# Layer step on one core: FFN sums and splits in another place, attention scores over 128 rows, sample keys and values as fp32 weights

## The chip, the cores and the metric

The kernel runs on one core of one Trainium2 chip. Its metric is the device time of one execution in microseconds (us). Before the change it takes 1013.33 us (median of three runs, 1012.04 to 1014.15).

## The reference

One inference step of a decoder layer with D = 1024, for a prompt of 512 tokens and 8 samples of one token each (520 columns in all):

```
x += 0.5 * (silu(h @ w1) * (h @ w3)) @ w2        # h = rmsnorm(x), hidden width 2816
z  = rmsnorm(x) @ w_in                           # conv gate b, c, x_in; attention q, k, v
y_c = b * causal_conv(c * x_in)                  # 512 channels
y_a = sum over 3 dilated windows, joint softmax of q k / 8, times v   # 8 heads x 64
x += concat(rmsnorm(y_c), rmsnorm(y_a)) @ w_out
x += 0.5 * (silu(h @ w1') * (h @ w3')) @ w2'
y  = rmsnorm(x)
```

A sample attends to 256 cached rows that the windows reach, and to itself; its keys and values come from the caches (`cache_k`, `cache_v`). The caches are also copied to the outputs, shifted by one row. All is fp32, and the products must keep fp32 accuracy.

## The kernel before, in words

Activations lie transposed: 128 channels on the partitions, the 520 tokens along the free axis, in two halves of 260. A large product is made from three fp32r matmuls (`mm3`, L121 to L123): both operands are split into a rounded part and a remainder (hi and lo), and hi·hi, hi·lo and lo·hi are added in PSUM. A weight block is loaded by `load_w` (L95): SyncE issues the DMA into one of four buffers `raw`, ScalarE rounds it to `hi` (L108), VectorE subtracts to get `lo` (L109). TensorE works nearly all the time; the other engines prepare operands for it.

The stages in order: first feed-forward block (0 to 380 us), mixer (380 to 644 us: projections, prompt heads, convolution, samples, output projection), second feed-forward block (644 to 1000 us), final norm.

*Feed-forward block* (`ffn`). Four hidden blocks m = 0 to 3 are made one by one from the split input `xh`, `xl` (the loop at L286): two products, the gate on ScalarE, `b` on VectorE (L302, L303), and the split into `hh` (ScalarE, L305) and `hl` (VectorE, L306). Then `down` (L311) multiplies them by w2 for the eight output blocks. After it come pairs of hidden blocks by `seven`, which needs sums of quarters of x: `x_sums(k)` (L350) makes, for k = 0 to 3, a tile `z` (names f0z, f1z; L355 to L359), its rounded part `sh` (ScalarE, L362) and its remainder `sl` (VectorE, L363, 128x1820). Two of the four calls, k = 0 and 1, stand behind m = 1 and m = 2 (L308); the other two, k = 2 and 3, stand inside the `down` loop (L311 to L314). A scheduler with a model of times puts the instructions of one engine in order; it may take work that is ready ahead of work that stands earlier in the code.

*Prompt heads* (`head`, L578). For each of eight heads, four blocks of 128 queries are multiplied by up to 512 keys. q is split into q2 (both halves of the 128 rows hold its 64 rounded rows) and ql (64 rows of remainder); k2 holds k's rounded rows in the head's half and its remainder in the other. One matmul over 128 rows gives q_hi·k_hi + q_hi·k_lo; a second one over 64 rows adds q_lo·k_hi (L589). The eight matmuls are kept in a fixed order.

*Samples.* Scores (`sample_scores`): for each of 8 samples the keys are loaded and split by `load_w`; the samples' queries stand in `sqm`, zero-padded 128x128 blocks that GpSimd fills and clears (L687, L689), as weights. 32 matmuls with 256 columns (L694) and 32 of 64 weight columns (L695) add all samples into one PSUM tile. Values (`sample_out`): the same with the probabilities as weights and the split values as the moving side, 16 + 16 matmuls of 512 columns (L741, L742), four transposes (L752), and sums into `AS` (L758, L759). Then `rstd_rows` (L813) and the second half of the output projection follow, which need the samples' result.

The order of the mixer's steps is the string `ORDER` (L33).

Of the kernel before, what the change touches and what calls it, by code (L numbers as in the profile page):

```python
# [16 lines left out]
B = 8  # L17
# [15 lines left out]
ORDER = ("A0 C00 C01! k1 q1 q2 B0 v1 v2 t1 C02 A1! B1! k3 k2 t2 A2 v3 C10 C11 q3 B2 t3 A3 C12 "  # L33
# [18 lines left out]
def tile_step(ctx: ExitStack, tc: tile.TileContext, xT, w0, w1a, w3a, w2a, w_in, w_out, w1b, w3b, w2b,  # L52
# [148 lines left out]
    def x_operand(pool, name, col, start):  # L201

        xh, xl = [], []
        for k in range(KD):
            h = pool.tile([P, T], F32R, name=f"{name}h{k}", tag=f"xh{k}")
            l = pool.tile([P, T], F32R, name=f"{name}l{k}", tag=f"xl{k}")
            for c in ([slice(0, TH), slice(TH, T)] if start and not k else [slice(0, T)]):
                scaled_split(X[k][:, c], h[:, c], l[:, c], col + k)
            xh.append(h)
            xl.append(l)  # L210
# [12 lines left out]
        A.activation(s, X[KD - 1], AF.Square)  # L223
        return xh, xl, sums + [s]

    def ffn(i, w1, w3, w2, g, psum, finish=None):
# [17 lines left out]
        with ExitStack() as st, ExitStack() as sx:  # L244
# [4 lines left out]
            with tc.tile_pool(name=f"xa{i}", bufs=1, side="right", reuse_waits="tile") as xa, \  # L249
# [36 lines left out]
                for m in range(CUTS[1]):  # L286
# [18 lines left out]
                    A.activation(hh, b, AF.Copy)  # L305
                    V.tensor_tensor(hl, b, hh.bitcast(F32), ALU.subtract)  # L306
# [170 lines left out]
    with ExitStack() as st:  # L477
# [9 lines left out]
        with ExitStack() as s2:  # L487
# [44 lines left out]

            qk, vs, vv = {}, {}, {}
# [23 lines left out]
            def do_q(hp):  # L557
                q = rotate(project(12 + hp), "q")
                G.tensor_copy(QS[:, hp], q[:, S:])
                q2 = [ap.tile([P, S], F32R, name=f"q2{e}", tag=f"q2{e}", bufs=2) for e in range(2)]  # L560
                ql = ap.tile([P, S], F32R, name="ql", tag="ql", bufs=2)
                for e in range(2):
                    for f in range(2):
                        A.activation(q2[e][ROWS[f]], q[ROWS[e], :S], AF.Copy)
                    V.tensor_tensor(ql[ROWS[e]], q[ROWS[e], :S], q2[e][ROWS[e]].bitcast(F32), ALU.subtract)
                qk["q", hp] = q2, ql
# [11 lines left out]
            def head(e, q2, ql, k2, v2, at):  # L578
# [5 lines left out]

                for at_, (ib, low) in enumerate(((0, 0), (1, 0), (0, 1), (1, 1), (2, 1), (2, 0), (3, 0), (3, 1))):
                    n = max(256, P * (ib + 1))
                    i = slice(ib * P, (ib + 1) * P)
                    one = ib < 2
                    mm = PE.matmul(dst[ib], lhsT=ql[rows, i] if low else q2[e][:, i], rhs=k2[e][rows if low else slice(0, P), :n],  # L589
                                   start=at_ in (0, 4, 6), stop=one or at_ in (5, 7), skip_group_check=one and at_ > 0)  # L590
                    if at_ not in (0, 6):
                        tc.keep_in_program_order(mm)
# [68 lines left out]
            def padded(n):  # L661

                z = [ap.tile([P, HP * 130 + 64], F32R, name=f"sqm{i}", tag=f"sqm{i}") for i in range(2)]
                for t in z:
                    G.memset(t[:, :n].bitcast(F32), 0.0)
                return z

            def sample_scores():
                zeros = padded(HP * 130 + 64)
# [6 lines left out]
                qs = ap.tile([P, B, HP, 2, 2], F32R, name="sqs", tag="sqs")  # L676
                A.activation(qs[:, :, :, 0], q2, AF.Copy)
                V.tensor_tensor(qs[:, :, :, 1], q2, qs[:, :, :, 0].bitcast(F32), ALU.subtract)
                sc = psS.tile([P, 512], F32, name="sc", tag="x", bufs=1)
                for b in range(B):  # L680
                    hi, lo = load_w(ckT[b], KD)
                    qf = zeros[b % 2]
                    for a in range(b % 2, b + 1, 2):
                        own = qf[:, NH * a:NH * a + 130 * HP].rearrange("p (h c) -> p h c", h=HP)[:, :, :P]
                        own = own.rearrange("p h (l c) -> p h l c", l=2)[:, :, :, :2]
                        if a == b:
                            G.tensor_copy(own, qs[:, b])  # L687
                        elif a == b - 2:
                            G.memset(own.bitcast(F32), 0.0)  # L689
                    qm = qf[:, :P * HP].rearrange("p (h l c) -> p h l c", h=HP, l=2)  # L690
                    for hp in range(HP):
                        k = slice(2 * hp, 2 * hp + 2)
                        end = b == B - 1 and hp == HP - 1
                        mm = [lambda: PE.matmul(sc[:, :256], lhsT=qm[:, hp], rhs=hi[:, k], start=b == 0 and hp == 0, stop=end),  # L694
                              lambda: PE.matmul(sc[:64, :256], lhsT=qm[:, hp, 0], rhs=lo[:, k], start=False, stop=False)]  # L695
                        for f in (mm[::-1] if end else mm):
                            f()
                    if b % 2 and b < B - 1:
                        yield
                PE.matmul(sc[:64, 256:257], lhsT=kq.rearrange("p b h e -> p (b h e)"), rhs=ones[:, 0:1], start=True, stop=True)  # L700
                got["sc"] = sc
                yield

            def sample_softmax(sc):
                ss = ap.tile([64, 257], F32, name="ss", tag="p2")
                V.memset(ss[:, 256:257], 0.0)
                A.activation(ss[:, :256], sc[64:, :256], AF.Copy)
                V.tensor_tensor(ss, sc[:64, :257], ss, ALU.add)
# [3 lines left out]
                V.tensor_tensor_reduce(out=pr, in0=ss, in1=smk, op0=ALU.add, op1=ALU.min, scale=-0.125, scalar=-NEG, accum_out=mx)  # L712
# [9 lines left out]
                return tp, pn  # L722

            def sample_out():
                tp, pn = got['m']
                zeros = padded(256)
                ps_ = ap.tile([P, 2, 2, 64], F32R, name="sps", tag="sqs")
                A.activation(ps_[:, :, 0], tp[:, :2], AF.Copy)
                V.tensor_tensor(ps_[:, :, 1], tp[:, :2], ps_[:, :, 0].bitcast(F32), ALU.subtract)
                so = psS.tile([P, 512], F32, name="so", tag="x", bufs=1)  # L730
                for b in range(B):
                    hi, lo = load_w(cvg[b], KD)
                    pz = zeros[b % 2][:, :256].rearrange("p (j l c) -> p j l c", j=2, l=2)
                    if b > 1:
                        G.memset(pz[:, :, :, NH * (b - 2):NH * (b - 1)].bitcast(F32), 0.0)
                    c = slice(NH * b, NH * (b + 1))
                    G.tensor_copy(pz[:, :, :, c], ps_[:, :, :, c])
                    for j in range(2):
                        k = slice(HP * j, HP * (j + 1))
                        end = b == B - 1 and j == 1  # L740
                        mm = [lambda: PE.matmul(so, lhsT=pz[:, j], rhs=hi[:, k], start=b == 0 and j == 0, stop=end),  # L741
                              lambda: PE.matmul(so[:64], lhsT=pz[:, j, 0], rhs=lo[:, k], start=False, stop=False)]  # L742
                        for f in (mm[::-1] if end else mm):
                            f()
# [5 lines left out]
                ot = psS.tile([P, 512], F32, name="ot", tag="s")  # L750
                for hp in range(HP):
                    PE.transpose(ot[:, 64 * hp:64 * hp + 64], os_[:, hp * P:(hp + 1) * P], ident[:64, :64])  # L752
                PE.matmul(ot[:, 320:384], lhsT=ones[:1, :], rhs=pn, start=True, stop=True)
                new = ot[:, 320:384].rearrange("p (b h e) -> p b h e", b=B, h=HP)
                own = ot[:, :66 * HP].rearrange("p (h c) -> p h c", h=HP)
                for e in range(2):
                    r = ROWS[e]
                    V.tensor_tensor(AS[r], new[r, :, :, e].rearrange("p b h -> p h b"), VS[r], ALU.mult)  # L758
                    V.tensor_tensor(AS[r], own[r, :, e:e + 8 * B - 7:8], AS[r], ALU.add)  # L759
# [26 lines left out]
            def go(step):  # L786
# [9 lines left out]
                elif what == "M":  # L796
                    got["m"] = sample_softmax(got["sc"])
# [165 lines left out]
```

## Time and profile before

| | |
|---|---|
| time, median of three runs | 1013.33 us (1012.04 to 1014.15) |
| the profiled execution | 1013.21 us, its span 1011.4 us |
| TensorE matmuls busy | 979.8 us, 97% of the span |
| weight loads busy | 956.2 us, 95% |
| VectorE busy | 719.8 us, 71% |
| ScalarE busy | 519.3 us, 51% |
| GpSimd busy | 69.5 us, 7% |
| mean DMA rate | 135 GB/s |

TensorE's matmuls are pipelined, so that their durations overlap: a matmul of 260 columns lasts 0.28 us in the profile, but the next starts 0.12 us after it. Costs on TensorE are therefore read from start to start. PEclk is the clock granted to TensorE, 1.00 for 2.4 GHz and 0.50 for 1.2 GHz. The fp32 matmuls (not fp32r) have two records each in the profile: the code's line 86 runs 8 of them at the start, and the profile counts 16.

### The profile page before, as it was taken

To read this page: it belongs to the slowest core of one execution; us is meant where nothing else is said; L and a number is where in the kernel's file an instruction comes from. 1 tells how busy PE (TensorE), PEld (TensorE's weight loads), DVE (VectorE), ACT (ScalarE), POOL (GpSimd) and SP (SyncE) were. 2 spreads that over 40 slices of the span, in tenths; PEclk is the share of its full clock that TensorE was granted. 3 is DMA by queue.
4 is the path that set the end of the run, shared out by engine and by line. 5 is a ranking of instruction groups with operands and counts; after the bars stand their busy time and mean duration, and the time that the engine had idled before them with its cause. 6 is when DMAs were issued, how large, how long until landed. Compare 5 with 4: busy or idle time off the path is not lost.

```text
span 1011.4 us, 19194 instructions
## 1 busy us (share of the span) xinstructions
PE 979.8 (97%) x7897; PEld 956.2 (95%) x7897; DVE 719.8 (71%) x1153; ACT 519.3 (51%) x941; POOL 69.5 (7%) x89
## 2 busy tenths in 40 slices
PE   8979999999999998999999999999999999999997
PEld 8979999999999998999999999999999999999997
DVE  7878888435886437676788889797898633788433
ACT  5535565423565325676476555453566522565442
POOL 1000000000000031111122220000000000000022
PEclk9989999999999999999999999999999999999998
DMA  7324434354444434233245466325444223333302
GB/s 240 109 93 168 146 135 143 108 179 168 147 146 146 138 134 164 105 127 130 102 146 209 159 223 223 116 93 168 145 146 147 60 87 125 106 100 110 105 21 86
DMA packets 37912, 136.62 MB, mean 135 GB/s; under 512 B 5760, under 2 KB 8512, under 8 KB 37312
## 3 DMA queue, kind: packets, MB, share of 16 engines
q1 hardware_dynamic: 37824, 135.39, 39.6%
q8 instruction: 62, 1.02, 0.4%
q14 instruction: 26, 0.21, 0.1%
HBM read 131.07 MB, written 37.82 MB: 167 GB/s over the span
## 4 chain that ended last, share of the span: by engine, by line
PE 75%; DVE 7%; issue 2%; DMA 2%; ACT 1%; POOL 1%; POOLq 0%; DVEq 0%; ACTq 0%
PE ps L121 24%; PE ps L123 23%; PE ps L122 23%; PE s L589 1%; DVE lo L390 1%; DVE lo L109 1%; DMA raw<-in_w1a 1%; PE pt L610 1%; DVE ls L390 1%; DMA raw<-in_w3a 1%; PE o L619 0%; ACT hi L108 0%; DVE raw L377 0%; ACT hi L389 0%; PE so L741 0%
## 5 line engine op out<-in xcount | busy, mean ns | idle before, releaser
L108 ACT ACTIVATE hi<-raw 128x1024 fp32r<-128x1024 f32 (+3 forms) x136 | 119.0, 878 | 214.2 <-PE ps L122 158.4
L121 PE MATMUL ps<-hh,hi 128*128 128x260 f32 x704 | 199.5, 286 | 5.6 <-ACT hh L305 3.1
L122 PE MATMUL ps<-hl,hi 128*128 128x260 f32 x704 | 199.2, 284 | 3.8 <-DVE hl L306 3.8
L123 PE MATMUL ps<-hh,lo 128*128 128x260 f32 x704 | 200.0, 285 | 2.8 <-DVE lo L109 2.8
L109 DVE TENSOR_TENSOR lo<-raw,hi 128x1024 fp32r<-128x1024 f32 (+3 forms) x136 | 138.6, 1020 | 74.4 <-ACT hi L108 73.3
L121 PEld LDWEIGHTS ps<-hh,hi 128*128 128x128 f32 x704 | 133.1, 190 | 7.4 <-ACT hh L305 3.5
L122 PEld LDWEIGHTS ps<-hl,hi 128*128 128x128 f32 x704 | 133.4, 190 | 4.5 <-DVE hl L306 4.5
L123 PEld LDWEIGHTS ps<-hh,lo 128*128 128x128 f32 x704 | 133.2, 189 | 3.9 <-DVE lo L109 3.4
L121 PE MATMUL ps<-mh,hi 128*128 128x260 f32 x384 | 110.0, 287 | 3.4 <-ACT mh L135 1.6
L122 PE MATMUL ps<-ml,hi 128*128 128x260 f32 x384 | 109.4, 285 | 0.8 <-DVE ml L136 0.8
L123 PE MATMUL ps<-mh,lo 128*128 128x260 f32 x384 | 109.1, 284 | 0.1
L389 ACT ACTIVATE hi<-raw 128x512 fp32r<-128x512 f32 x144 | 82.5, 621 | 35.9 <-PE ps L122 26.6
L390 DVE TENSOR_TENSOR lo<-raw,hi 128x1024 fp32r<-128x1024 f32 x72 | 87.7, 1218 | 5.3 <-ACT hi L389 4.8
L121 PE MATMUL ps<-f0sh,hi 128*128 128x260 f32 x288 | 81.5, 284 | 1.4 <-ACT hi L389 1.0
L121 PE MATMUL ps<-f1sh,hi 128*128 128x260 f32 x288 | 81.3, 283 | 0.4 <-ACT a L401 0.3
L123 PE MATMUL ps<-f0sh,lo 128*128 128x260 f32 x288 | 80.7, 284 | 0.9 <-DVE lo L390 0.7
L123 PE MATMUL ps<-f1sh,lo 128*128 128x260 f32 x288 | 80.9, 284 | 0.1
L122 PE MATMUL ps<-f0sl,hi 128*128 128x260 f32 x288 | 81.0, 282 | 0.0
L122 PE MATMUL ps<-f1sl,hi 128*128 128x260 f32 x288 | 81.0, 282 | 0.0
L144 POOL TENSOR_TENSOR acc<-acc,sq 128x520 f32<-128x520 f32 (+1 forms) x19 | 28.7, 1511 | 750.4 <-ACT sq L143 750.4
L121 PEld LDWEIGHTS ps<-mh,hi 128*128 128x128 f32 x384 | 72.2, 188 | 4.8 <-ACT mh L135 1.9
L122 PEld LDWEIGHTS ps<-ml,hi 128*128 128x128 f32 x384 | 72.3, 188 | 2.2 <-DVE ml L136 1.0
(278 smaller groups left out, 2660.2 us busy)
## 6 DMA issues: line engine op xcount, KB each, us to landing
out_cko<-in_ck SPq DMA_DIRECT2D x16, 1023.0 KB, 6.1
out_cvo<-in_cv SPq DMA_DIRECT2D x16, 1023.0 KB, 7.6
raw<-in_w_in SPq DMA_DIRECT2D x24, 512.0 KB, 3.3
raw<-in_w1b SPq DMA_DIRECT2D x22, 512.0 KB, 3.3
raw<-in_w3b SPq DMA_DIRECT2D x22, 512.0 KB, 3.3
raw<-in_w3a SPq DMA_DIRECT2D x21, 512.0 KB, 3.3
raw<-in_w1a SPq DMA_DIRECT2D x20, 512.0 KB, 3.3
raw<-in_w2a SPq DMA_DIRECT2D x16, 320.0 KB, 3.0
```

Of the source, the lines that this page charges most:

```text
L108: A.activation(hi, raw, AF.Copy)
L109: V.tensor_tensor(lo, raw, hi.bitcast(F32), ALU.subtract)
L121: PE.matmul(out, lhsT=hi, rhs=xh, start=start, stop=False, skip_group_check=more)
L122: PE.matmul(out, lhsT=hi, rhs=xl, start=False, stop=False, skip_group_check=more)
L123: PE.matmul(out, lhsT=lo, rhs=xh, start=False, stop=stop, skip_group_check=more)
L144: eng.tensor_tensor(dst[:, c], dst[:, c], sq[:, c], ALU.add)
L389: A.activation(h[:, c:c + KQ], f[:, c:c + KQ], AF.Copy)
L390: V.tensor_tensor(l, f, h.bitcast(F32), ALU.subtract)
L589: mm = PE.matmul(dst[ib], lhsT=ql[rows, i] if low else q2[e][:, i], rhs=k2[e][rows if low else slice(0, P), :n], start=at_ in (0, 4, 6), s ...
L610: PE.transpose(t[:, o + ib * P:o + (ib + 1) * P], pr[ib][:, jb * P:(jb + 1) * P], ident)
```

## The change

There are four parts.

1. In `x_operand` the tiles of the split input are allocated ahead of their use, in reversed order.
2. In `ffn`, the sums of x for k = 2 and 3 are issued after both halves of the last hidden split (m = 3) instead of wherever the scheduler finds room.
3. In `head`, the remainder matmul runs over 128 rows. Four tiles `rest` hold ql in one half and zeros (written once) in the other. The matmuls of one block of queries stand next to each other, without a kept order. In `ORDER`, B0 moves ahead of q2.
4. In the samples, keys and values are used as they come from the DMA, as fp32 weights (128x128 blocks of `raw`), with two moving columns (the two heads of a pair) each: 64 matmuls for the scores (8 samples x 4 pairs x 2 halves), 64 for the values. `load_w`, the padded tiles on GpSimd and the split of the probabilities go. The scores come out transposed: two transposes turn them back, and the values need none.

```diff
-ORDER = ("A0 C00 C01! k1 q1 q2 B0 v1 v2 t1 ...
+ORDER = ("A0 C00 C01! k1 q1 B0 q2 v1 v2 t1 ...
...
     def x_operand(pool, name, col, start):
-        xh, xl = [], []
+        xs = [[pool.tile([P, T], F32R, name=f"{name}{x}{k}", tag=f"x{x}{k}") for x in "hl"] for k in range(KD)[::-1]]
+        xh, xl = zip(*xs[::-1])
...
                     hh, hl = hidden(m)
-                    A.activation(hh, b, AF.Copy)
-                    V.tensor_tensor(hl, b, hh.bitcast(F32), ALU.subtract)
+                    made = [A.activation(hh, b, AF.Copy), V.tensor_tensor(hl, b, hh.bitcast(F32), ALU.subtract)]
...
                     if then:
-                        then()
+                        with tc.issue_after(made[0].ins), tc.issue_after(made[1].ins):
+                            then()
...
+            rest = [[ap.tile([P, S], F32R, name=f"ql{i}{e}") for e in range(2)] for i in range(2)]
+            for r in rest:
+                for e in range(2):
+                    V.memset(r[e][ROWS[1 - e]].bitcast(F32), 0.0)
...
-                for at_, (ib, low) in enumerate(((0, 0), (1, 0), (0, 1), (1, 1), (2, 1), (2, 0), (3, 0), (3, 1))):
+                for ib in range(4):
                     n = max(256, P * (ib + 1))
                     i = slice(ib * P, (ib + 1) * P)
-                    mm = PE.matmul(dst[ib], lhsT=ql[rows, i] if low else q2[e][:, i], rhs=k2[e][rows if low else slice(0, P), :n],
...
+                    PE.matmul(dst[ib], lhsT=q2[e][:, i], rhs=k2[e][:, :n], start=True, stop=False)
+                    PE.matmul(dst[ib], lhsT=ql[e][:, i], rhs=k2[e][:, :n], start=False, stop=True)
...
+            def cache(src):
+                raw = wp.tile([P, KD, P], F32, name="raw", tag="raw", bufs=4)
+                load(raw, src)
+                return raw
...
                 for b in range(B):
-                    hi, lo = load_w(ckT[b], KD)
...
+                    raw = cache(ckT[b])
                     for hp in range(HP):
...
-                        mm = [lambda: PE.matmul(sc[:, :256], lhsT=qm[:, hp], rhs=hi[:, k], start=b == 0 and hp == 0, stop=end),
-                              lambda: PE.matmul(sc[:64, :256], lhsT=qm[:, hp, 0], rhs=lo[:, k], start=False, stop=False)]
+                        for j in range(2):
+                            PE.matmul(sc[:, j, b, hp], lhsT=raw[:, 2 * hp + j], rhs=q2[:, b, hp], start=True, stop=True)
...
+                for j in range(2):
+                    PE.transpose(ss[:64, j * P:(j + 1) * P], st[:, j], ident)
...
-                        mm = [lambda: PE.matmul(so, lhsT=pz[:, j], rhs=hi[:, k], start=b == 0 and j == 0, stop=end),
-                              lambda: PE.matmul(so[:64], lhsT=pz[:, j, 0], rhs=lo[:, k], start=False, stop=False)]
+                    raw = cache(cvg[b])
+                    for hp in range(HP):
+                        for j in range(2):
+                            PE.matmul(so[:, j, b, hp], lhsT=raw[:, HP * j + hp], rhs=pj[:, j, b, hp], start=True, stop=True)
...
-                os_ = ap.tile([64, 512], F32, name="os_", tag="u")
-                A.activation(os_, so[64:], AF.Copy)
-                V.tensor_tensor(os_, so[:64], os_, ALU.add)
...
-                    V.tensor_tensor(AS[r], own[r, :, e:e + 8 * B - 7:8], AS[r], ALU.add)
+                    for j in range(2):
+                        V.tensor_tensor(AS[r], so[r, j, :, :, e].rearrange("p b h -> p h b"), AS[r], ALU.add)
```

The lines of the changed kernel have other numbers: in the loop of the hidden blocks they are lower by 2 or 3 (L306 is L303), the scores stand in L591 and L592, the samples' products in L678 and L715.

The order of VectorE where the first feed-forward block ends its hidden blocks; hl_581 is the remainder of m = 2, hl_711 that of m = 3, f0sl the remainders of the sums. Before:

```order
L303 TENSOR_TENSOR b<-b,a 128x520
L358 SCALAR_TENSOR_TENSOR f0z<-f0z 128x260 x2
L359 SCALAR_TENSOR_TENSOR f0z<-f0z 128x260 x2
L306 TENSOR_TENSOR hl_581<-b,hh_580 128x520
L302 TENSOR_TENSOR b<-ps,rbc 128x520
L303 TENSOR_TENSOR b<-b,a 128x520
L363 TENSOR_TENSOR f0sl_753<-f0z,f0sh_752 128x1820
L363 TENSOR_TENSOR f0sl_828<-f0z,f0sh_827 128x1820
L306 TENSOR_TENSOR hl_711<-b,hh_710 128x520
```

And of the changed kernel:

```order
L301 TENSOR_TENSOR b<-b,a 128x520
L109 TENSOR_TENSOR lo<-raw,hi 128x512
L303 TENSOR_TENSOR hl_581<-b,hh_580 128x520
L300 TENSOR_TENSOR b<-ps,rbc 128x520
L301 TENSOR_TENSOR b<-b,a 128x520
L303 TENSOR_TENSOR hl_711<-b,hh_710 128x520
L353 SCALAR_TENSOR_TENSOR f0z<-X_70,gv,rbc 128x520
L353 SCALAR_TENSOR_TENSOR f0z<-X_66,gv,rbc 128x520
L353 SCALAR_TENSOR_TENSOR f0z<-X_71,gv,rbc 128x520
L353 SCALAR_TENSOR_TENSOR f0z<-X_67,gv,rbc 128x520
```

The making of the sums and their two long remainders stood ahead of hl_711; now all of it stands behind hl_711, and the remainders come between the updates of X in `down`.

The order of TensorE at the scores of the first head; s01, s2 and s3 are PSUM tiles. Before, with the 64-row matmuls reading ql:

```order
L589 MATMUL s01_4681<-k20_4661,q20_4592 128x256 x2
L589 MATMUL s01_4681<-k20_4661,ql_4594 128x256 x2
L589 MATMUL s2_4682<-k20_4661,ql_4594 128x384
L589 MATMUL s2_4682<-k20_4661,q20_4592 128x384
L589 MATMUL s3_4683<-k20_4661,q20_4592 128x512
L589 MATMUL s3_4683<-k20_4661,ql_4594 128x512
```

And of the changed kernel, where ql00 has 128 rows:

```order
L591 MATMUL s01_4688<-k20_4668,q20_4600 128x256
L592 MATMUL s01_4688<-k20_4668,ql00_4479 128x256
L591 MATMUL s01_4688<-k20_4668,q20_4600 128x256
L592 MATMUL s01_4688<-k20_4668,ql00_4479 128x256
L591 MATMUL s2_4689<-k20_4668,q20_4600 128x384
L592 MATMUL s2_4689<-k20_4668,ql00_4479 128x384
L591 MATMUL s3_4690<-k20_4668,q20_4600 128x512
L592 MATMUL s3_4690<-k20_4668,ql00_4479 128x512
```

The same eight products remain; the two kinds alternate, and none has fewer than 128 rows.

The order of TensorE at the end of the samples' values; so is the PSUM tile of the result, sqm the padded probabilities, raw the loaded values. Before:

```order
L742 MATMUL so_6700<-lo_6970,sqm0_6693 64x512
L741 MATMUL so_6700<-hi_6969,sqm0_6693 128x512
L742 MATMUL so_6700<-lo_6970,sqm0_6693 64x512
L741 MATMUL so_6700<-hi_6981,sqm1_6694 128x512
L619 MATMUL o_6801<-pth0_4469,v2_6030 128x512
```

And of the changed kernel, where spj holds the probabilities:

```order
L715 MATMUL so_6647<-spj_6582,raw_6885 128x2 x5
L715 MATMUL so_6647<-spj_6582,raw_6895 128x2 x5
L618 MATMUL o_6746<-ptl3_4476,v2_6034 64x256
L619 MATMUL o_6746<-pth3_4472,v2_6034 128x256
L715 MATMUL so_6647<-spj_6582,raw_6895 128x2 x3
L715 MATMUL so_6647<-spj_6582,raw_6905 128x2 x8
L715 MATMUL so_6647<-spj_6582,raw_6915 128x2 x8
L719 MATMUL ot_6925<-spn_6580,ones_73 128x64
```

A few products of 512 columns between others have become a run of 29 products of two columns. Elsewhere the changed order has such runs of 16 (scores), 16 and 2 (values, followed by the five products of L193), and 17 among transposes. Behind ot, the changed order has 35 matmuls of the output projection ahead of the norm that needs the samples; before it has 72 of them.

## Rows read from the trace of the kernel before

**Rows 1.** The page's first section: busy time, share of the span, instructions of each engine

```profile
PE 979.8 (97%) x7897; PEld 956.2 (95%) x7897; DVE 719.8 (71%) x1153; ACT 519.3 (51%) x941; POOL 69.5 (7%) x89
```

**Rows 2.** Busy time by stretch; columns: stretch, length, engines, clock, DMA share, GB/s

```profile
412.00:600.00 188.00, 187.36 (x1429) 174.82 (x1429) 145.96 (x308) 116.20 (x221) 32.96 (x55) 1.00 0.44 152
```

**Rows 3.** TensorE in order of time, first feed-forward block; columns: start, us, work, [idle before]

```profile
59.28 0.62 PE L121 MATMUL ps<-hh,hi 128*128 128x260 f32 x3 [1.14 <-ACT hh L305]
60.57 0.39 PE L122 MATMUL ps<-hl,hi 128*128 128x260 f32 x1 [0.67 <-DVE hl L306]
63.51 1.02 PE L121 MATMUL ps<-hh,hi 128*128 128x260 f32 x3 [1.95 <-ACT hh L305]
66.58 0.59 PE L122 MATMUL ps<-hl,hi 128*128 128x260 f32 x1 [2.05 <-DVE hl L306]
```

**Rows 4.** VectorE in order of time, the same stretch

```profile
61.90 4.01 DVE L363 TENSOR_TENSOR f0sl<-f0z,f0sh 128x1820 fp32r<-128x1820 f32 x2
65.83 0.69 DVE L306 TENSOR_TENSOR hl<-b,hh 128x520 fp32r<-128x520 f32 x1
70.02 0.70 DVE L427 SCALAR_TENSOR_TENSOR X<-ps,X 128x520 f32<-128x520 f32 x1 [3.50 <-PE ps L123]
```

**Rows 5.** TensorE in order of time, the same place of the second block

```profile
683.88 0.39 PE L123 MATMUL ps<-hh,lo 128*128 128x260 f32 x1 [1.57 <-DVE lo L109]
686.46 0.39 PE L122 MATMUL ps<-hl,hi 128*128 128x260 f32 x1 [1.10 <-DVE hl L306]
```

**Rows 6.** VectorE in order of time, just before

```profile
683.75 2.05 DVE L363 TENSOR_TENSOR f1sl<-f1z,f1sh 128x1820 fp32r<-128x1820 f32 x1
```

**Rows 7.** TensorE in order of time, the scores of one head

```profile
417.45 0.40 PE L589 MATMUL s<-k,q 128*128 128x256 f32 x2
418.98 0.50 PE L589 MATMUL s<-k,ql 64*128 64x512 f32 x1
419.40 0.39 PE L121 MATMUL ps<-mh,hi 128*128 128x260 f32 x1
```

**Rows 8.** TensorE in order of time, sample values and projection

```profile
590.15 0.40 PE L741 MATMUL so<-hi,sqm 128*128 128x512 f32 x1
590.38 0.39 PE L742 MATMUL so<-lo,sqm 128*64 128x512 f32 x1
592.70 0.28 PE L121 MATMUL ps<-Yh,hi 128*128 128x260 f32 x1
592.82 0.28 PE L122 MATMUL ps<-Yl,hi 128*128 128x260 f32 x1
```

**Rows 9.** Waits of the removed line 741

```profile
  POOL sqm L737: 0.8, 2
```

**Rows 10.** TensorE in order of time, fp32 products

```profile
573.88 1.08 PE L193 MATMUL nps<-ones,acc 128*104 128x1 f32 x10 [0.20 <-POOL acc L144]
574.81 0.37 PE L589 MATMUL s<-k,q 128*128 128x256 f32 x1
999.99 1.05 PE L86 MATMUL ps<-ones 128*128 128x128 f32 x8
1000.88 0.58 PE L839 MATMUL nps<-ones,acc 128*65 128x1 f32 x8
```

**Rows 11.** Busy time by stretch where the clock fell

```profile
60.00:63.40 3.40, 0.99 (x6) 0.78 (x6) 3.33 (x4) 3.40 (x3) 0.00 (x0) 1.00 0.05 19
66.80:70.20 3.40, 3.40 (x16) 3.40 (x17) 0.18 (x1) 0.35 (x1) 0.00 (x0) 0.50 0.00 0
1002.10:1005.50 3.40, 3.10 (x29) 2.91 (x30) 0.99 (x6) 0.87 (x3) 0.00 (x0) 1.00 0.61 202
1005.50:1008.90 3.40, 0.84 (x5) 0.65 (x4) 1.75 (x6) 0.39 (x1) 1.42 (x2) 0.50 0.63 215
```

**Rows 12.** VectorE and ScalarE in order of time, end of the samples

```profile
600.53 0.20 DVE L759 TENSOR_TENSOR AS<-ot,AS 64x32 f32<-64x32 f32 x1
603.51 0.64 ACT L171 ACTIVATE rhi<-acc_a 128x520 fp32r<-128x520 f32 x1 [0.32 <-POOL acc_a L144]
```

More of the change, by code (lines that the diff above doesn't have):

```diff
@@ L560, in do_q @@
                 q2 = [ap.tile([P, S], F32R, name=f"q2{e}", tag=f"q2{e}", bufs=2) for e in range(2)]
-                ql = ap.tile([P, S], F32R, name="ql", tag="ql", bufs=2)
+                ql = rest[hp % 2]
                 for e in range(2):
@@ L675, in sample_scores @@
                 V.tensor_tensor(kq, q2, KS.rearrange("p h b -> p b h").unsqueeze(3).to_broadcast([P, B, HP, 2]), ALU.mult)
[L676 to L679, printed above, removed]
+                sc = psS.tile([P, 2, B, HP, 2], F32, name="sc", tag="x", bufs=1)
@@ L680, in sample_scores @@
                 for b in range(B):
-                    hi, lo = load_w(ckT[b], KD)
[L682 to L689, printed above, removed]
@@ L698, in sample_scores, with sample_softmax @@
+                    for hp in range(HP):
+                        for j in range(2):
+                            PE.matmul(sc[:, j, b, hp], lhsT=raw[:, 2 * hp + j], rhs=q2[:, b, hp], start=True, stop=True)
                     if b % 2 and b < B - 1:
                         yield
-                PE.matmul(sc[:64, 256:257], lhsT=kq.rearrange("p b h e -> p (b h e)"), rhs=ones[:, 0:1], start=True, stop=True)
-                got["sc"] = sc
+                got["sc"] = sc, kq
                 yield
[L704 to L708, printed above, removed]
+            def sample_softmax(sc, kq):
+                st = ap.tile([P, 2, 64], F32, name="st", tag="p2")
+                A.activation(st, sc.rearrange("p j b h e -> p j (b h e)"), AF.Copy)
+                ss = psS.tile([P, 512], F32, name="ss", tag="s")
+                for j in range(2):
+                    PE.transpose(ss[:64, j * P:(j + 1) * P], st[:, j], ident)
+                PE.matmul(ss[:64, 256:257], lhsT=kq.rearrange("p b h e -> p (b h e)"), rhs=ones[:, 0:1], start=True, stop=True)
@@ L721, in sample_softmax @@
                 V.tensor_copy(pn, tp[:1, 2])
-                return tp, pn
+                pj = ap.tile([P, 2, B, HP, 2], F32, name="spj")
+                V.tensor_copy(pj.rearrange("p j b h e -> p j (b h e)"), tp[:, :2])
+                return pj, pn
             def sample_out():
[L725 to L729, printed above, removed]
@@ L730, in sample_out @@
-                so = psS.tile([P, 512], F32, name="so", tag="x", bufs=1)
-                for b in range(B):
[L732 to L740, printed above, removed]
-                        mm = [lambda: PE.matmul(so, lhsT=pz[:, j], rhs=hi[:, k], start=b == 0 and j == 0, stop=end),
-                              lambda: PE.matmul(so[:64], lhsT=pz[:, j, 0], rhs=lo[:, k], start=False, stop=False)]
-                        for f in (mm[::-1] if end else mm):
-                            f()
+                pj, pn = got['m']
@@ L748, in sample_out @@
-                A.activation(os_, so[64:], AF.Copy)
-                V.tensor_tensor(os_, so[:64], os_, ALU.add)
[L750 to L754, printed above, removed]
@@ L755, in sample_out @@
-                own = ot[:, :66 * HP].rearrange("p (h c) -> p h c", h=HP)
+                ot = psS.tile([P, B, HP, 2], F32, name="ot", tag="s")
+                PE.matmul(ot.rearrange("p b h e -> p (b h e)"), lhsT=ones[:1, :], rhs=pn, start=True, stop=True)
                 for e in range(2):
                     r = ROWS[e]
-                    V.tensor_tensor(AS[r], new[r, :, :, e].rearrange("p b h -> p h b"), VS[r], ALU.mult)
-                    V.tensor_tensor(AS[r], own[r, :, e:e + 8 * B - 7:8], AS[r], ALU.add)
+                    V.tensor_tensor(AS[r], ot[r, :, :, e].rearrange("p b h -> p h b"), VS[r], ALU.mult)
+                    for j in range(2):
+                        V.tensor_tensor(AS[r], so[r, j, :, :, e].rearrange("p b h -> p h b"), AS[r], ALU.add)
@@ L796, in go @@
                 elif what == "M":
-                    got["m"] = sample_softmax(got["sc"])
+                    got["m"] = sample_softmax(*got["sc"])
                 elif what == "V":
```

28 lines of the change are left out of this document (5 added, 23 removed).

## The prediction

> **What bounds the kernel now.** I read the page's busy line first, then busy time by stretch, then TensorE in order of time wherever a stretch is not full. TensorE's matmuls are busy 979.8 of 1011.4 us [rows 1], and in the mixer's middle, where most of the change lies, 187.36 of 188.00 us at a granted clock of 1.00, while VectorE has 145.96 and ScalarE 116.20 [rows 2]. So a change there is worth what it does to TensorE's own list, from start to start; work taken off ScalarE, VectorE and GpSimd (32 splits of the samples' keys and values, the padded tiles) is worth nothing, being hidden by that list, except where TensorE waited for it. A GEMM matmul of 260 columns costs 0.12 us and one of 512 columns 0.23 us [rows 8].
>
> The visible holes in TensorE's time lie at the end of the hidden blocks. In the first feed-forward block TensorE waits 1.14, 0.67, 1.95 and 2.05 us, for hh and hl [rows 3]. The VectorE rows say why: two long remainders f0sl, 4.01 us, start at 61.90, and hl of the last hidden block gets its turn only at 65.83 [rows 4]. TensorE worked 0.99 us of 60.00 to 63.40, and the granted clock then stood at 0.50, that is 1.2 GHz: 66.80 to 70.20 holds 16 matmuls [rows 11], where 3.40 us at 0.12 us would hold 28. In the second block the waits are 1.57 and 1.10 us [rows 5], again with a 2.05 us remainder just ahead of hl [rows 6], and without a fall of the clock.
>
> **The change, part by part.** The sum is made against the profiled execution, 1013.21 us (a span of 1011.4 and 1.8 around it), 0.1 below the median of 1013.33.
>
> *Part 1* only changes where tiles lie: 0.
>
> *Part 2, first block.* The four waits make 5.81 us, and I add an estimated 1.2 us for refilling the pipeline behind each (0.39 instead of 0.28 us for the first matmul [rows 3, 7], some 0.3 us for each start that was late). The slow clock costs (28 - 16) x 0.12 = 1.5 us. That is 8.5 us. In the new order hl of m = 3 follows directly on its product b, with no remainder between. I expect it done near 59.9, with about 1 us of waiting left for the chain product, gate, split. Gain 7.5. If the new order only shortens the last two waits (4.0 us) it is 4; if nothing is left waiting it is 8.5. The moved work, about 9 us of VectorE (four products for the sums, four 260- or 520-column passes, 4.01 us of remainders), needs cover: VectorE idles 3.50 us until 70.02 in the down stage [rows 4], and the rest must fit between the updates of X, before the pairs need the sums. That is tight, so I put 0.3 us of new waits against it, with 0 and 3 as ends.
>
> *Part 2, second block.* 1.57 + 1.10 = 2.67 us, with the refills 3.0; 0.3 stays. Gain 2.7 (1 to 3). Together part 2 gives -7.5 - 2.7 + 0.3 = -9.9 us.
>
> *Part 3.* One head's scores take from 417.45 to 419.40, and the GEMM behind them another 0.11 us more than usual: 2.06 us. The 64-row matmul of 512 columns alone takes 0.42 us until the next start [rows 7] against 0.23 us for 512 columns elsewhere [rows 8]. Eight 128-row matmuls at the usual pace are 4 x 0.12 + 2 x 0.175 + 2 x 0.23 = 1.29 us (0.175 for 384 columns lies between the two measured). So -0.77 us per head and, for eight heads, -6.2 us. Ends: 0, if the alternation keeps the cost, and -7. The zeros are written once on VectorE, four passes over 64 rows, beside a full TensorE: 0. The Trainium skill (TensorE: Matmul & The Clock Gate, section "Why this matters for your kernels") holds that a single matmul over few rows takes the same time as one over 128; by that rule this part would give 0 and the sum below would be 6.2 us higher. The row disagrees: 0.42 against 0.23 us.
>
> *Part 4, TensorE.* Removed are 64 matmuls of 256 columns and 32 of 512: 64 x 0.12 + 32 x 0.23 = 15.0 us, and the wait of 0.8 us for GpSimd's padded tile [rows 9]. Added are 128 fp32 matmuls with 128 weight columns and two moving columns, each with two records. No row shows exactly this. The nearest is L193, fp32 with 104 weight columns and one moving column: ten records from 573.88 to 574.81, 0.093 us each; by weight columns that makes 0.114. L86, 128 weight columns, takes 0.89 / 8 = 0.111 us a record [rows 10]. I take 0.112, because one moving column cannot be what costs 0.093 us, so the weights set the pace: 2 x 128 x 0.112 = 28.7 us. Ends: 23.8 us at 0.093, and 57 us if all of it ran at half clock. The transposes (four removed, two added) about cancel. Part 4 so far: 28.7 - 15.8 = +12.9.
>
> *Part 4, its end.* Behind the samples, the norm of the attention output needs AS. In the trace AS is done at 600.73 and the sum of its squares is read from 603.51 on [rows 12]; 2.8 us; then come the two split halves, 0.64 us on ScalarE [rows 12] and, as for hl [rows 4], 0.69 on VectorE, and ahead of it six small VectorE operations of up to 0.2 us [rows 12], about 1.0: 5.1 us. The new order leaves 35 matmuls, 4.2 us, as cover where there were 72. About 0.9 us new wait (0 to 2).
>
> Sum at full clock: -9.9 - 6.2 + 12.9 + 0.9 = -2.3 us, 1010.9.
>
> *Part 4, the clock.* This decides. From 1002.10 to 1005.50 TensorE was busy 3.10 of 3.40 us and its weight loads 2.91, with almost nothing but fp32 matmuls on few columns (L839 with one column, L86, L160), and the granted clock in the next stretch is 0.50. In the GEMM code the fall came behind a stretch in which it was busy 0.99 us [rows 11]. So being busy with fp32 weight loads did not hold the clock there. The ten records of L193, 0.93 us, did not lower it [rows 2, 10]; but the new order has runs of 16 (3.6 us), 16 + 2 + L193 (5 us), 17 among transposes (5 us), and 10 + 19 (6.5 us). The fall in the first block lasted from about 63.4, where the stretch at 1.00 ends, to 70.2, 6.8 us, and at 16 matmuls for 28 a busy TensorE loses 6.8 x 12/28 = 2.9 us in it. Three falls of the four runs: estimated 8.5 us. Bounds: 0 for none, 17 for six of them. I take 8.5, as the one row in which TensorE runs such work for over 3 us shows the fall. The sum is 1010.9 + 8.5 = 1019.4; I say 1019.
>
> The Trainium skill (same page, Part 1: The HAM clock gate) describes the gate as following how busy the engine has recently been; read as time in which it executes, as the busy columns have it, TensorE would stay at 2.4 GHz through the new runs, and the result is the 1010.9 of the sum at full clock. The row from 1002.10 on speaks against that reading, though it also holds 0.3 us of idleness and follows a wait.
>
> **Rivals.**
> *No fall.* The fp32 runs keep the clock, and the kernel is faster: 1010.9, with the ends of the terms 1007 to 1013. For it: L193's run passed unharmed, and the runs lie between dense GEMMs. Against it: the row just named.
> *One fall.* Only the run of 29 brings it on: 1010.9 + 2.9 = 1013.8, no difference. It is the break-even: each fall eats more than the whole net gain of 2.3 us.
> *The scores stay at their old cost,* because what delays them is not the 64 rows but the change of operands: +6.2, 1017 without a fall. Against it: the 128-row matmuls of that head, two in 0.33 us, come close to pace [rows 7].
> *The moved sums arrive late at the pairs,* and the gain of part 2 shrinks from 9.9 to about 5: 1016 without a fall, 1024 with three.
>
> **How the numbers follow.** Within 0.2% (2 us) a change can't be told from none, so "same" is 1011.3 to 1015.4. Two or more falls: 0.50 (own range 1014 to 1024, nearly all of it slower). No fall: 0.32, five sixths of it faster, the rest same. One fall: 0.11, mostly same. Scores or sums without their gain and no fall: 0.07, slower or same. That makes faster 0.30, same 0.17, slower 0.53. The range goes from 1007, the good end of the sum at full clock, to 1024, where three falls meet one more or a late sum.
>
> **What would show it.** Part 2: the waits for hh and hl around 58 to 67 gone but for about 1 us, the clock 1.00 through the down stage, and VectorE's f0sl done by about 76. Part 3: about 1.3 us for a head's eight matmuls. Part 4: 0.112 us from record to record in L678 and L715, 256 records; GpSimd gone from TensorE's releasers; a wait of about a microsecond at the norm behind ot. The clock: stretches at 0.50 inside or right behind the runs of L678 and L715. I am wrong if the clock column stays at 1.00 from 520 to 610 us, or if a record of these lines takes clearly other than 0.11 us at full clock.

## The result, and the profile after

The changed kernel takes 1030.9 us (median of four runs, 1027.61 to 1032.43) against 1013.74 of the kernel before in the same comparison: 1.0155 times, 95% interval 1.0116 to 1.0193. The forecast was 1019 with a range to 1024. The direction was right, the size was not: the loss is 17 us instead of 6. The profiled execution is the fastest of the four, 1027.61 us.

The page of the changed kernel, the busy line and the granted clock in 40 slices, answers to [rows 1]:

```profile
PE 1000.1 (97%) x8055; PEld 988.9 (96%) x8055; DVE 702.5 (68%) x1139; ACT 504.2 (49%) x922; POOL 58.9 (6%) x57
...
PEclk9999999999999989999988969999999999999998
```

TensorE is busy 20 us longer, all other engines work less, and the clock row has dents past its middle that the kernel before does not have. Busy time by stretch (columns as in [rows 2]) of the changed kernel:

```profile
57.50:70.50 13.00, 11.98 (x99) 11.56 (x97) 11.71 (x22) 4.96 (x7) 0.00 (x0) 1.00 0.55 185
372.00:385.50 13.50, 8.59 (x54) 8.18 (x53) 10.75 (x20) 7.18 (x11) 0.00 (x0) 0.75 0.29 95
500.00:620.00 120.00, 119.43 (x844) 117.66 (x843) 61.92 (x145) 42.39 (x95) 13.34 (x13) 0.83 0.44 152
```

The first row is part 2's gain: 11.98 us of 13.00 busy at full clock, where the kernel before had holes and half clock [rows 3, 11]. The last row is the loss: TensorE is busy throughout, but at a mean clock of 0.83, which is 41 us of the 120 at 1.2 GHz (120 x 0.17 x 2). The middle row is a second loss, at the start of the mixer.

Where the clock falls, the same view in short stretches shows it. Three of seven falls, each with the stretch ahead of it:

```profile
511.80:515.20 3.40, 3.40 (x30) 3.31 (x29) 2.65 (x9) 1.64 (x5) 0.00 (x0) 1.00 0.07 18
515.20:518.60 3.40, 3.40 (x17) 3.40 (x18) 1.95 (x7) 1.87 (x3) 0.00 (x0) 0.50 0.54 187
...
552.70:556.20 3.50, 3.50 (x34) 3.50 (x32) 0.70 (x1) 0.00 (x0) 0.00 (x0) 0.99 1.15 441
556.20:559.60 3.40, 3.40 (x17) 3.40 (x17) 0.17 (x1) 0.91 (x2) 0.00 (x0) 0.50 0.43 125
...
600.50:603.90 3.40, 3.40 (x33) 3.40 (x32) 1.22 (x2) 0.59 (x1) 0.00 (x0) 1.00 0.94 332
603.90:607.30 3.40, 3.40 (x18) 3.40 (x18) 1.72 (x2) 1.76 (x3) 1.27 (x1) 0.51 0.46 141
```

TensorE and its weight loads are busy for the whole of the stretch ahead, and the clock falls all the same. TensorE in order of time says what it was busy with; here the last scores and the last values:

```profile
553.40 4.31 PE L678 MATMUL sc<-sq,raw 128*128 128x2 f32 x32
557.57 0.57 PE L121 MATMUL ps<-mh,hi 128*128 128x260 f32 x1
557.93 0.42 PE L122 MATMUL ps<-ml,hi 128*128 128x260 f32 x1
...
599.40 2.29 PE L715 MATMUL so<-spj,raw 128*128 128x2 f32 x20
...
601.83 6.16 PE L715 MATMUL so<-spj,raw 128*128 128x2 f32 x38
```

The 32 records of L678 are 16 products; from the fall on, a GEMM matmul lasts 0.42 instead of 0.28 us. The other four falls lie at the end of the other groups of L678 and L715 or right behind them (at 532.3, 545.9, 580.1 and 590.3 us): every group has one.

The scores of one head, TensorE in order of time, answer to [rows 7]:

```profile
411.15 0.28 PE L591 MATMUL s<-k,q 128*128 128x256 f32 x1
411.27 0.28 PE L592 MATMUL s<-k,ql 128*128 128x256 f32 x1
...
411.96 0.40 PE L591 MATMUL s<-k,q 128*128 128x512 f32 x1
412.20 0.39 PE L592 MATMUL s<-k,ql 128*128 128x512 f32 x1
```

All eight now keep pace: 412.20 - 411.15, and 0.23 for the last, is 1.28 us for a head where it was 2.06.

The weight loads show what the 64 rows had cost. A weight load of the kernel before and one of the changed kernel, PEld in order of time:

```profile
418.97 0.18 PEld L589 LDWEIGHTS s<-k,ql 64*128 64x128 f32 x1 [0.30 <-issue]
```

```profile
411.97 0.19 PEld L592 LDWEIGHTS s<-k,ql 128*128 128x128 f32 x1
```

Before, the load starts together with its own matmul (418.98 [rows 7]); in the changed kernel it starts 0.23 us ahead of its matmul at 412.20, beside the one before. In the trace of the kernel before, load and matmul start together at each of the 40 changes between 128 and 64 rows around the scores. Where one 64-row matmul of 256 columns follows another (418.00 us), the load is ahead, and the next matmul comes after 0.12 us, as behind one on 128 rows. So the cost lies in the changes of the number of rows, not in the few rows.

### The profile page after: what moved, and what is told of

It reads as the page before. It is cut to its first block, busy times and chain, and to the rows that moved or that the text cites. A ratio compares the mean times of both kernels' runs of the same rounds, so it can differ in the third digit from the quotient of the medians.

```text
span 1025.8 us, 19401 instructions
## 1 busy us (share of the span) xinstructions
PE 1000.1 (97%) x8055; PEld 988.9 (96%) x8055; DVE 702.5 (68%) x1139; ACT 504.2 (49%) x922; POOL 58.9 (6%) x57
## 4 chain that ended last, share of the span: by engine, by line
PE 88%; DVE 5%; DMA 3%; ACT 2%; issue 2%; SPq 0%; POOL 0%; POOLq 0%; DVEq 0%; ACTq 0%
PE ps L121 27%; PE ps L123 27%; PE ps L122 27%; PE so L715 2%; PE sc L678 1%; DVE lo L388 1%; PE pt L610 1%; ACT hi L108 1%; DMA raw<-in_w1a 1%; DMA raw<-in_w1b 1%; DVE lo L109 1%; DMA X<-in_xT 1%; PE s L591 1%; PE o L619 1%; PE s L592 0%
## 5 line engine op out<-in xcount | busy, mean ns | idle before, releaser
L108 ACT ACTIVATE hi<-raw 128x1024 fp32r<-128x1024 f32 (+3 forms) x120 | 102.3, 853 | 210.2 <-PE ps L122 158.4
L109 DVE TENSOR_TENSOR lo<-raw,hi 128x1024 fp32r<-128x1024 f32 (+3 forms) x120 | 115.8, 966 | 88.8 <-ACT hi L108 88.7
L121 PE MATMUL ps<-mh,hi 128*128 128x260 f32 x384 | 114.2, 298 | 2.8 <-ACT mh L135 1.6
L122 PE MATMUL ps<-ml,hi 128*128 128x260 f32 x384 | 113.6, 296 | 3.3 <-DVE ml L136 3.3
L123 PE MATMUL ps<-mh,lo 128*128 128x260 f32 x384 | 113.3, 295 | 0.0
L122 PEld LDWEIGHTS ps<-ml,hi 128*128 128x128 f32 x384 | 76.5, 199 | 3.9 <-DVE ml L136 3.5
L121 PEld LDWEIGHTS ps<-mh,hi 128*128 128x128 f32 x384 | 76.5, 199 | 3.7 <-ACT mh L135 1.9
L123 PEld LDWEIGHTS ps<-mh,lo 128*128 128x128 f32 x384 | 76.6, 199 | 0.5
```

The costliest lines, as they stand in the source:

```text
L108: A.activation(hi, raw, AF.Copy)
L109: V.tensor_tensor(lo, raw, hi.bitcast(F32), ALU.subtract)
L121: PE.matmul(out, lhsT=hi, rhs=xh, start=start, stop=False, skip_group_check=more)
L122: PE.matmul(out, lhsT=hi, rhs=xl, start=False, stop=False, skip_group_check=more)
L123: PE.matmul(out, lhsT=lo, rhs=xh, start=False, stop=stop, skip_group_check=more)
```

## The experiments

Seven kernels were run, two of them twice.

**Part 2 alone** (with part 1, which only places tiles):

```diff
+        xs = [[pool.tile(...) for x in "hl"] for k in range(KD)[::-1]]
...
+                        with tc.issue_after(made[0].ins), tc.issue_after(made[1].ins):
+                            then()
```

> Parts 1 and 2 alone (tile order in x_operand, sums of x behind the last hidden split), the rest as before. Theory A (the sum of the prediction holds for this part, the loss of the changed kernel is the samples' clock): 10 to 13 us faster than before, about 1002, the waits for hh and hl at 58 to 67 us down to about 1 us. Rival B (the gain is given back later, at the pairs or at the start of the mixer, where the changed kernel shows a new stretch at half clock from 375 us): 4 to 7 us faster, with a stretch at 0.50 near 375.

Measured: 1004.49 us against 1013.99, ratio 0.9909 (0.9883 to 0.9934), so -9.5 us: between the two theories, just below the 10 to 13 us of A and above the 4 to 7 us of B. The waits at the hidden blocks went as A says, down to one of 0.91 us. But a part of the gain is given back, as B says, at the pairs of hidden blocks and at the start of the mixer. Busy time by stretch of this kernel:

```profile
113.00:137.00 24.00, 24.00 (x201) 23.96 (x201) 20.19 (x31) 14.29 (x32) 0.00 (x0) 1.00 0.42 150
145.00:172.00 27.00, 24.33 (x198) 23.69 (x198) 20.00 (x33) 14.33 (x31) 0.00 (x0) 1.00 0.32 110
```

and of the kernel before:

```profile
113.00:137.00 24.00, 22.05 (x178) 21.22 (x176) 19.67 (x30) 14.48 (x31) 0.00 (x0) 1.00 0.43 153
145.00:172.00 27.00, 26.97 (x225) 26.76 (x224) 24.58 (x38) 17.91 (x38) 0.00 (x0) 1.00 0.36 121
```

Holes of 1.95 us in the first stretch go, and 2.67 us come in the second, where TensorE now waits for `lo` and for VectorE's additions at the second pair. Lined up GEMM matmul by GEMM matmul with the kernel before, this one is 7.8 us ahead at 70 us, 9.5 at 138 and 6.0 at 172 (times of the kernel before). At the start of the mixer it loses another 1.5 us in a stretch at half clock that the kernel before does not have:

```profile
378.00:383.00 5.00, 4.32 (x23) 4.32 (x24) 5.00 (x8) 4.18 (x7) 0.00 (x0) 0.66 0.38 109
```

**Part 3 alone.** The samples' padded tiles need the memory that the zeros want, so the mask and the small sample tiles share a buffer of q, k and v:

```diff
+            rest = [[ap.tile([P, S], F32R, name=f"ql{i}{e}") ...
+                    PE.matmul(dst[ib], lhsT=ql[e][:, i], rhs=k2[e][:, :n], start=False, stop=True)
...
-            smk = ap.tile([64, 257], F32, name="smk")
+                both = ap.tile([P, 336], F32, name="smk", tag="qkv", bufs=2)
```

> Part 3 alone: scores over 128 rows with zeros and B0 ahead of q2, the samples as before. To make room, the samples' mask, queries and split probabilities share a buffer of q, k and v, and the mask is loaded later. Theory A (64-row matmuls start late): 16.6 us of score matmuls become about 10.5, 5 to 6 us faster, about 1008. Rival B (a single matmul over 64 rows costs what one over 128 does): no difference.

Measured: 1010.88 us against 1013.99, ratio 0.9967 (0.9950 to 0.9983): -3.1 us, between the two theories. The heads are as fast as forecast; from 404 us, in front of most heads, to 587 us the kernel gains 6.2 us on the one before (the same GEMM matmul stands 1.8 us later there, and 4.4 us earlier here). But 2.9 us are lost ahead of the heads, at the start of the mixer. The rows of the same wait are in the run of zeros on GpSimd below. What B0 ahead of q2 does was not run by itself.

**Part 4 alone**, parts 1 to 3 left out:

```diff
+                    raw = cache(ckT[b])
+                            PE.matmul(sc[:, j, b, hp], lhsT=raw[:, 2 * hp + j], rhs=q2[:, b, hp], start=True, stop=True)
```

> Part 4 alone: keys and values as fp32 weights with two moving columns, the rest as before. Theory A (the runs of these products lower the clock): about 14 us more at full clock and some 35 to 45 us of stretches at 0.50 between 515 and 625 us, each losing 12/28 of its length, so 29 to 33 us slower, 1043 to 1047. Rival B (the falls in the changed kernel come from its other parts, which leave the engine short of other matmuls there): no falls, 12 to 15 us slower, about 1027.

Measured: 1046.68 us against 1013.99, ratio 1.0323 (1.0306 to 1.0340): +32.7 us. Theory A holds, and the other parts are not the cause of the falls. The stretch of the samples in this kernel:

```profile
500.00:640.00 140.00, 140.00 (x928) 133.94 (x927) 71.98 (x168) 49.64 (x110) 13.79 (x14) 0.80 0.38 134
```

A mean clock of 0.80 over 140 us is 56 us at half clock; at 12/28 that is 24 us, and 14 us for the products at full clock make 38. That is above the difference of the medians, but the profiled execution is the slowest of six, 39 us above the profiled one before.

**Parts 1 to 3 without part 4:** the kernel of the two short diffs for parts 2 and 3 together.

> Parts 1 to 3 without part 4: the samples as before, with the room made as in the run of part 3 alone. Theory A: the gains add up, 10 + 6 us, about 998, no stretch at half clock between 500 and 620 us; this would be faster than both kernels. Rival B (TensorE finds no work in place of what went, the gains overlap): 1003 to 1008.

Measured: 1001.11 us against 1013.99, ratio 0.9878 (0.9861 to 0.9895): -12.9 us, faster than both kernels, with 1.00 as the clock from 500 to 620 us. The two gains alone, 9.5 and 3.1, add up to 12.6. It missed the 998 by 3.1 us; lined up as above, its trace loses 5.5 us on the kernel before between 384 and 392 us, at the start of the mixer.

**128 moving columns instead of two.** The moving operand is widened to the right, by the next pairs' columns and by zeros; the surplus results are overwritten by the later products:

```diff
-                            PE.matmul(sc[:, j, b, hp], lhsT=raw[:, 2 * hp + j], rhs=q2[:, b, hp], start=True, stop=True)
+                            at = NH * b + 2 * hp
+                            PE.matmul(scw[:, j, at:at + 128], lhsT=raw[:, 2 * hp + j], rhs=qw[:, at:at + 128], start=True, stop=True)
```

> The changed kernel with 128 moving columns instead of 2 in each of the samples' 128 products: the moving side is the same tile from the pair's column on, and the surplus columns are overwritten by the products that follow. The weights, their number, their order and the runs are as in the changed kernel. Theory A (what lowers the clock is the few moving columns): a record still takes about 0.112 us, no stretch at 0.50 between 500 and 620 us, 16 to 18 us faster than the changed kernel, about 1013. Rival B (fp32 weight loads lower the clock, whatever moves): the falls stay, 1031. Rival C (the products cost by their moving columns after all): a record takes 0.2 us or more, 1035 or above at full clock.

Measured: 1014.28 us against 1014.57, ratio 0.9995 (0.9976 to 1.0013), 16.6 us below the changed kernel (about 17.5 if each is set against the kernel before in its own comparison). Theory A holds; B and C fall. The same stretch, and the same last scores, of this kernel:

```profile
500.00:620.00 120.00, 119.71 (x998) 117.94 (x997) 76.83 (x170) 51.18 (x110) 14.52 (x14) 1.00 0.49 172
```

```profile
552.71 3.74 PE L681 MATMUL sc<-sq,raw 128*128 128x128 f32 x32
556.20 0.37 PE L121 MATMUL ps<-mh,hi 128*128 128x260 f32 x1
```

The same 32 records on the same weights take 3.49 us to the next start, 0.109 us each, with 64 times as many columns moving, and the clock stays at 1.00. In the changed kernel they took 4.17 us because the clock fell on the way. Where it had not fallen yet, the cost is the same; the first values, in the changed kernel:

```profile
574.87 3.63 PE L715 MATMUL so<-spj,raw 128*128 128x2 f32 x32
578.36 0.49 PE L121 MATMUL ps<-Yh,hi 128*128 128x260 f32 x2
```

and with 128 columns:

```profile
571.07 3.73 PE L721 MATMUL so<-spj,raw 128*128 128x128 f32 x32
574.55 0.49 PE L121 MATMUL ps<-Yh,hi 128*128 128x260 f32 x2
```

That is 3.49 and 3.48 us; behind the first the clock falls at 580.1, behind the second it does not fall. The scheduler did not put all products in the same groups in the two kernels. Three of the seven groups, the first and last scores and the first values, stand alike in both traces, and the clock falls at each of them with 2 columns and at none with 128. The second and third groups of the scores stand here much as in the run of part 4 alone, where both fell.

**The products spread.** Each score product is put behind one triple of GEMM matmuls, and the values, with a changed `ORDER` behind O1, among the triples of the output blocks:

```diff
                 mm3(ps[:, h, :TH], hi, lo, xh[k][:, c], xl[k][:, c], i == 0, i == len(ks) - 1)
+                for _ in range(rate[0]):
+                    if trickle:
+                        trickle.pop(0)()
```

> The changed kernel with the samples' products spread: each of the 64 score products stands behind one hi-hi, hi-lo, lo-hi triple of a projection, and the values are spread over output blocks O0 to O5 as far as the order of the steps lets them (many stay in runs). Two moving columns and all weights as in the changed kernel. Theory A (the clock falls where such products stand closely together): the four falls between 515 and 563 us, which follow the score products, go, some 20 us at 0.50 or 8.8 us of time; the falls at the values stay; about 1021 to 1024. Rival B (any such product costs the clock something, spread or not): stretches at 0.50 also among the spread scores, 1029 or more.

Measured: 1030.41 us (1023.44 to 1037.66) against 1013.19, ratio 1.0148 (1.0069 to 1.0227), no faster than the changed kernel. At the scores the clock does what theory A says; the time is that of B (1029 or more), for other reasons. Busy time by stretch of this kernel, through the scores:

```profile
516.90:527.50 10.60, 10.60 (x92) 10.51 (x91) 5.84 (x18) 4.65 (x11) 0.00 (x0) 1.00 0.15 49
...
540.00:544.50 4.50, 4.50 (x42) 4.50 (x41) 4.43 (x10) 1.25 (x3) 1.30 (x1) 1.00 0.91 335
544.50:547.90 3.40, 3.40 (x15) 2.90 (x14) 1.50 (x2) 1.53 (x3) 1.31 (x2) 0.50 0.67 260
547.90:563.00 15.10, 14.96 (x127) 14.75 (x126) 3.97 (x5) 2.71 (x3) 0.00 (x0) 1.00 0.49 181
```

and TensorE's order of time, where the scheduler had put products together again, and at two later places:

```profile
541.75 1.62 PE L687 MATMUL sc<-sq,raw 128*128 128x2 f32 x14
...
570.26 0.63 PE L699 MATMUL ss<-ident,st 128*64 128x128 f32 x2 [4.63 <-ACT st L696]
...
637.07 0.56 PE L121 MATMUL ps<-Yh,hi 128*128 128x260 f32 x1 [2.77 <-DVE t L749]
```

Of four falls among the scores one is left, behind the one place where 24 records, or 12 products, stand close together (540 to 543 us). Spread singly, from 547.9 to 563.0 us and before 527.5, the same products leave the clock at 1.00. The time is lost elsewhere: the scores now end just ahead of the softmax, whose transposes wait 4.63 us, with a fall behind them; the values, most of which stayed in runs, have three falls (at 582.0, 595.7 and 616.2 us); and an output block waits 2.77 us.

**Zeros on GpSimd**, in the kernel with parts 1 to 3:

```diff
-                    V.memset(r[e][ROWS[1 - e]].bitcast(F32), 0.0)
+                    G.memset(r[e][ROWS[1 - e]].bitcast(F32), 0.0)
```

> Parts 1 to 3 with the samples as before, and the zeros of the score tiles written by GpSimd instead of VectorE. In the run of parts 1 to 3 alone the four memsets took 2.37 us on VectorE at the start of the mixer, just ahead of the first ml, for which TensorE then waited 3.25 us, and the clock fell. Theory A: ml comes 2.4 us earlier, the wait is about 0.8 us as in the kernel before, and 2 to 5 us go (5 if the clock does not fall): 996 to 999. Rival B (the mixer's first products then wait for something else, such as the weights' split): 1000 to 1001.

Measured: 1001.35 us (999.79 to 1003.5) against 1013.19, ratio 0.9870 (0.9830 to 0.9911), no better than with the zeros on VectorE (0.9878). The wait behaved as forecast, but its profiled execution, the slowest of the four, has a fall at 165.7 us and one at 380.7. So both kernels were run again on one chip.

> The kernel with parts 1 to 3 alone once more (zeros on VectorE), on the same chip as the next one, to tell a difference of 2 us between the two. Theory A (the memsets cost 2.4 us at the start of the mixer): 2 to 4 us slower than the next kernel. Rival B (other waits and falls of the clock decide): no difference, both about 1001.

> Parts 1 to 3 with the zeros on GpSimd once more, in five rounds. Theory A: 2 to 4 us faster than with the zeros on VectorE, 997 to 999. Rival B: no difference.

Measured: 1000.80 us (998.98 to 1001.92) with the zeros on VectorE, 997.99 us (996.2 to 1001.52) with them on GpSimd; against 1015.53 of the kernel before, 0.9856 (0.9834 to 0.9877) and 0.9833 (0.9809 to 0.9858). The medians differ by 2.8 us the way of theory A, but the intervals overlap, and the first pair of runs showed no difference: a gain in time is not shown. The mechanism is plain in the traces. Zeros on VectorE, its order of time and TensorE's:

```profile
374.52 2.37 DVE L534 MEMSET ql<- 64x512 f32 x4
376.83 1.21 DVE L109 TENSOR_TENSOR lo<-raw,hi 128x1024 fp32r<-128x1024 f32 x1
...
377.96 5.44 DVE L136 SCALAR_TENSOR_TENSOR ml<-X,gv,mh 128x520 fp32r<-128x520 f32 x8
```

```profile
378.77 0.58 PE L122 MATMUL ps<-ml,hi 128*128 128x260 f32 x1 [3.25 <-DVE ml L136]
```

Zeros on GpSimd, its order of time and TensorE's:

```profile
373.74 2.24 POOL L534 MEMSET ql<- 64x512 f32 x4
```

```profile
379.00 0.39 PE L122 MATMUL ps<-ml,hi 128*128 128x260 f32 x1 [0.80 <-DVE ml L136]
```

The memsets stood in front of the first remainder that the mixer needs; moved away, TensorE waits 0.80 instead of 3.25 us. Every trace here bears that out. Lined up with the kernel before, the six traces with the zeros on VectorE lose 4.2 to 6.0 us between 384 and 392 us; the two with them on GpSimd lose 1.5 and 0.0, the two without them (part 2 alone, part 4 alone) 1.5 each. In the time this is mixed with what the second pair costs in each execution: from 70 to 180 us the four traces with parts 1 to 3 give back 0.4 and 0.5 us (zeros on VectorE), 1.9 and 3.7 (on GpSimd). The kernel with the zeros on GpSimd is 11.8 us ahead of the one before in its first run and 17.5 in its second.

## Why the prediction was right and wrong

*The clock: right in kind, wrong in size.* The failing step is "Three falls of the four runs: estimated 8.5 us". There were seven falls and 41 us at half clock; at 12/28 that is 17.6 us, and the run with 128 moving columns, which has no fall there, is 16.6 us faster. The 9 us by which this exceeds my 8.5 are most of the 12 us by which the time exceeds the forecast. The count was wrong rather than the length: a fall lasted 5.9 us on average where I had taken 6.8. I had counted only long unbroken runs in the order, four of them, and passed over three groups of the scores, 16 products each with a few others between. Every group fell, and the last one stayed at half clock for 10 us. My bound of 17 us for six falls was about the truth, but I took the middle, and the range's end of 1024 left it out. That the kernel would be slower, and by the clock, was right.

The Trainium skill (TensorE: Matmul & The Clock Gate, Part 1: The HAM clock gate) has the gate follow how busy the engine has been. Read as time busy in the profile's columns, that is refuted here: 3.40 of 3.40 us busy, and 1.2 GHz next. With 128 columns moving, on the same weights and at the same busy time (119.71 us of 120 against 119.43), the clock stayed at 2.4 GHz. The groups that stand alike in both traces differ in the moving columns alone, so these decide here.

*Part 4 at full clock* was forecast at +12.9 and +0.9 us. The kernels with part 4 on wide columns and without part 4 differ by 1014.28 - 1001.11 = 13.2 us, or 12.6 if each is set against the kernel before in its own comparison. A record takes 0.109 us for the 0.112 taken. The 0.9 us of waiting at the norm behind the samples did not come; L178 shows no wait in either kernel.

*Part 3* was right for the heads (1.28 us for 1.29), but the row of 0.42 us was misread. It was set against the Trainium skill's rule of equal time for few rows (same page, "Why this matters for your kernels"), which speaks of a single matmul. The trace agrees with the rule where 64-row matmuls of 256 columns follow each other: 0.12 us at 418.00, as on 128 rows. What made eight matmuls take 2.06 us are the four changes between 64 and 128 rows in that head, an estimated 0.19 us each, from (2.06 - 1.28) / 4. Wrong was "The zeros are written once on VectorE, four passes over 64 rows, beside a full TensorE: 0". The code stands in the mixer, but the scheduler put the memsets where TensorE is not full but waits for VectorE. In the changed kernel, VectorE in order of time:

```profile
373.40 2.37 DVE L535 MEMSET ql<- 64x512 f32 x4
...
376.86 2.75 DVE L136 SCALAR_TENSOR_TENSOR ml<-X,gv,mh 128x520 fp32r<-128x520 f32 x4
```

and TensorE:

```profile
377.65 0.58 PE L122 MATMUL ps<-ml,hi 128*128 128x260 f32 x1 [3.26 <-DVE ml L136]
```

That is 2.4 us of waiting more than the 0.81 us in the kernel before, and the clock was at 0.50 from 375.3 to 382.1. The wide-column run (1014.3) misses my sum at full clock (1010.9) by 3.4 us; its trace loses 6.0 us at this place, so the other terms, taken together, came out better than forecast.

*Part 2* was forecast at -9.9 us and measured at -9.5. Its first waits shrank as forecast: of 5.81 us one wait of 0.91 is left, TensorE in the changed kernel,

```profile
59.02 0.63 PE L121 MATMUL ps<-hh,hi 128*128 128x260 f32 x3 [0.91 <-ACT hh L303]
```

and the second remainder of the sums (L361) ends at 75.6 us, as expected by 76. That the waits at the pairs would change places I had only as a bound of 3 us; in the run of part 2 alone they give back 1.8 us between 70 and 180 us.

Not settled: how often the clock falls where TensorE waits at the start of the mixer and at the second pair. Two executions of the very same kernel, with the zeros on GpSimd, show it at both places in one and at neither in the other.

## What to carry to other kernels

Before weights are used unsplit with a handful of moving columns, count all such products, also those in groups broken by a few others: here every group of 16 to 29 products took the clock to half, and that cost more (17 us) than the products themselves added (13 us). A record took the same time with 128 moving columns as with 2, so widening the moving operand cost nothing here and held the clock. Spread singly among GEMM matmuls the products held it too, but that run was no faster in all. Even with the clock held, the unsplit weights did not pay: the kernel with parts 1 to 3 and the samples as before takes 1001.1 us. Where matmuls on 64 and on 128 rows alternate, look at the weight loads: here the changes of the row number cost, not the small matmuls. A memset that is "written once" still has a place in an engine's order: look where the scheduler puts it; here it delayed TensorE's first operand by 2.4 us, and on GpSimd it did not.

## What the runs showed that was not expected

An fp32 record with 128 weight columns costs 0.109 us with 128 moving columns, and 0.109 with 2. A TensorE that is busy for 119.43 of 120 us was clocked down to 1.2 GHz seven times in 100 us. A change between 64 and 128 rows kept the next weight load from starting ahead of its matmul, at all 40 of them. And one kernel's executions differ with nothing changed: 996.2 to 1001.5 us with the zeros on GpSimd, 1023.4 to 1037.7 with the products spread.
